# Handing the small products of a hybrid HGRN2 and retention layer to TensorE at other places in the program

## The chip, the cores and the metric

The kernel runs on one core of one Trainium2 chip. The core has TensorE (PE, matrix products), VectorE (DVE), ScalarE (ACT), GpSimd (POOL) and SyncE (SP, which here issues the DMAs). The time is device microseconds of the core for one execution of the whole program.

## The reference

One decoder layer over L = 2048 tokens of width D = 1024, in fp32. The hidden state is normalized and modulated by c, projected once into ten parts, and two recurrent mixers with 8 heads each work on them: HGRN2 (a linear recurrence with a decay f for each channel) and retention (a fixed decay for each head, with rotated q and k). Each output is normalized by head, gated, and the two are merged, projected back and added.

```python
mod = silu(c) @ w_ada + b_ada
shift, scale, gate = split(mod, 3)
h = rms_norm(x, norm_g) * (1 + scale) + shift
hq, hf, hi, hz, rq, rk, rv, rz, ga, gb = split(h @ w_in)
f = lb + (1 - lb) * sigmoid(hf);  k = 1 - f;  q = silu(hq)
oA: S_t = diag(f_t) S_(t-1) + k_t hi_t^T,   o_t = S_t^T q_t
oB: R_t = gamma R_(t-1) + rot(rk)_t rv_t^T, o_t = R_t^T rot(rq)_t
uA = head_rms_norm(oA) * silu(hz);  uB = head_rms_norm(oB) * silu(rz)
x = x + gate * ((sigmoid(ga) * uA + sigmoid(gb) * uB) @ w_out)
out = rms_norm(x, final_g)
```

## The kernel before

**Tiling.** The tokens are worked in NSB = 2 superblocks of 1024, each in two blocks of 512 or eight chunks of 128 (CH = 8). The heads go in NP = 4 pairs. For every superblock and pair PE runs dense projections in groups of 24 matmuls (8 steps along D, three matmuls of a split fp32 product each, `mm3`): `gf` and `gq` (weights a: f and q of HGRN2), `gr` (weights b: q and k of retention, for two pairs at once, so only in even pairs), `gv` (weights c: the values of both), `gg` (weights d: the gates). The first pair runs c, a, b, d; the others a, b (even pairs), c, d. At the end stands the output projection `ops`. Dense results go through three PSUM buffers (`gg0`, `gg1` ... name heads, the second number a chunk). Weights come by DMA (`wa` to `wd`, two raw tiles of 512 KB in flight); ACT copies the high part (`whd` ...), DVE subtracts the low part (`wld` ..., L464); `Ring` does both and keeps the last subtraction in `self.last`.

**Small products** are handed to PE between the dense ones. `Background` counts a tick at each step of three dense matmuls; after GAP = 9 ticks (27 dense matmuls) it makes a burst, in which each lane, a generator, may put its next piece: `tree` (L554) the seven levels `lv` 1, 2, 4 ... 64 of the products within a block of HGRN2, with the masked copies into `af`; `hgrn_out` (L683) the outputs and state updates `poh`; `retention` (L784) a chunk's scores `rt`, its output `por` and state. A lane that is not ready says so and the burst goes on without it. `bg.since` sets how far the count stands when a stage begins. `bg.post(w, fn)` calls fn w ticks later: it is used to issue DMAs when their operands should be there. `side` lanes (`block_r`, the row norms of a coming block) get a step every four ticks. PE keeps program order (`PE.on`); the other engines are ordered by the scheduler, unless `tc.issue_after(x)` puts instructions behind x on their engine.

**What the steps below touch.** After the last tree level, k times the decay is transposed on DVE (L645), stored to DRAM (`dk`, L657) and fetched back (`k<-dk`, eight DMAs, L650); `us` hands it to `hgrn_out` once `age[bb] + 6` ticks are past (L664). `rotate` (L742) turns q and k of a chunk: two multiplications that read the accumulator `gr` (L749), add and subtract (L757, L758), a transpose (L760), `kz` (L762), and `send`, which stores them 4 ticks later; it stands behind `ring.last`, the newest weight split. `retention` fetches them (`fetch`, L797, L798) up to one chunk ahead, again by a post of 4 ticks, into NQP = 3 buffers. `ada_row` (L176) makes a half of the output gate: eight multiply-adds on DVE (L189), then a matmul with ones, `gps`. `block_h` and `split_h` (L345) make the normalized h tiles of a block (high part L350 or L352, low part L353); those of block 2 are made while the last gates of superblock 0 run, in the `hook` (L1008) that is called behind each group. `gates` (L847) and `merge` (L857) are DVE's work behind each `gg` group.

## Time and profile before

| | |
|---|---|
| time, median of 3 runs | 2093.68 us (2092.19 to 2094.02) |
| the profiled execution's own time | 2095.28 us |
| span of its instructions | 2093.5 us |
| mean granted clock of PE | 0.992 |
| PE idle within the span | 2093.5 - 2039.0 = 54.5 us |
| DMA, mean over the span | 90 GB/s |

The busy time of an engine is what its records cover; a busy PE need not run at its full clock, so the clock granted to it is read beside it. In a list of waits, the engine named behind the arrow ended the wait. A row of the timeline gives the start, the length, the engine, the line, the operation, the result and operands, and in brackets the idle time of the engine before it with what ended it.

### The profile page before, as it was taken

Reading aid. Unit: us, or ns where it says so; the run is one execution under the profiler, and the core shown is the slowest. Engines: PE = TensorE matmul, PEld = TensorE weight load, DVE = VectorE, ACT = ScalarE, POOL = GpSimd, SP = SyncE. Lnnn points to the kernel's source line nnn. Section 1 sums busy time; section 2 is a strip of 40 time slices with the busy share of each in tenths; the row PEclk is TensorE's granted clock in tenths of the full one; section 3 lists DMA queues with packets and bytes.
Section 4 is the critical chain, followed back from the end, with each engine's and each line's share of the span. In section 5 each row is a group of like instructions: output and inputs, shape, how many; then the busy total and the mean of one; then the engine's idle time right before and its main releaser. Section 6 shows DMA issues by size and latency. Waiting matters only on the chain.

```text
span 2093.5 us, 38260 instructions
## 1 busy us (share of the span) xinstructions
PE 2039.0 (97%) x15448; PEld 1670.1 (80%) x15448; DVE 1086.0 (52%) x2435; ACT 572.5 (27%) x1389; POOL 145.9 (7%) x274
## 2 busy tenths in 40 slices
PE   6998999999999999999999999999999999999998
PEld 4786888788887887787888887888888887877886
DVE  7366544554365534556565544553464535465543
ACT  6312322322113221334213222322123222323221
POOL 1000100010000100121000100010000100110000
PEclk9999999999999999999999999999999999999999
DMA  8135221422244221435244221422344211447531
GB/s 314 41 75 124 63 72 46 93 57 56 60 118 96 68 54 47 103 93 154 56 102 97 67 55 46 97 56 53 73 99 94 72 47 53 100 113 203 176 131 60
DMA packets 312560, 187.66 MB, mean 90 GB/s; under 512 B 217664, under 2 KB 274496, under 8 KB 312384
## 3 DMA queue, kind: packets, MB, share of 16 engines
q1 hardware_dynamic: 312384, 185.22, 33.1%
q8 instruction: 121, 1.98, 0.4%
q14 instruction: 55, 0.45, 0.1%
HBM read 147.39 MB, written 37.75 MB: 88 GB/s over the span
## 4 chain that ended last, share of the span: by engine, by line
PE 52%; DMA 1%; DVE 1%; issue 1%; ACT 0%; POOL 0%; SPq 0%; DVEq 0%; POOLq 0%; ACTq 0%
PE gg L52 17%; PE gv L52 8%; PE ops L52 8%; PE gr L52 4%; PE gq L52 4%; PE gf L52 4%; PE poh L52 2%; PE lv L52 2%; PE por L52 1%; PE rt L52 1%; DMA wd<-in_w_d_dram 0%; DMA wc<-in_w_c_dram 0%; DMA mT_dram<-ga 0%; DMA wg<-in_w_gate_dram 0%; DMA wa<-in_w_a_dram 0%
## 5 line engine op out<-in xcount | busy, mean ns | idle before, releaser
L52 PE MATMUL gg<-whd,h 128*128 128x512 f32 x2048 | 658.6, 395 | 1.1 <-DVE tr L749 1.1
L52 PEld LDWEIGHTS gg<-whd,h 128*128 128x128 f32 x2048 | 386.6, 189 | 80.6 <-issue 1.9
L52 PE MATMUL gg<-wld,h 128*128 128x512 f32 x1024 | 400.3, 391 | 0.1
L52 PE MATMUL gv<-whc,h 128*128 128x512 f32 x1024 | 332.3, 397 | 3.5 <-ACT v L889 2.1
L52 PEld LDWEIGHTS gv<-whc,h 128*128 128x128 f32 x1024 | 192.5, 188 | 45.9 <-ACT v L889 3.3
L52 PEld LDWEIGHTS gg<-wld,h 128*128 128x128 f32 x1024 | 193.6, 189 | 38.8 <-DVE wld L464 0.5
L52 PE MATMUL gv<-wlc,h 128*128 128x512 f32 x512 | 199.0, 391 | 1.2 <-DVE wlc L464 1.1
L52 PE MATMUL gf<-h,wha 128*128 128x512 f32 x512 | 159.4, 392 | 2.4 <-DVE h L352 1.3
L52 PE MATMUL gr<-whb,h 128*128 128x512 f32 x512 | 160.3, 391 | 0.0
L52 PE MATMUL gq<-h,wha 128*128 128x512 f32 x512 | 158.6, 391 | 0.0
L52 PE MATMUL ops<-wo,mh 128*128 128x512 f32 x512 | 157.5, 389 | 0.0
L115 POOL TENSOR_TENSOR rrr<-ssr,mhalf 128x2 f32<-128x2 f32 x64 | 51.4, 803 | 1202.1 <-DVE ssr L114 1145.2
L850 ACT ACTIVATE sgg<-gg 128x512 f32<-128x512 f32 x128 | 74.8, 594 | 209.5 <-PE gg L52 206.9
L464 DVE TENSOR_TENSOR wld<-wd,whd 128x512 fp32r<-128x512 f32 x128 | 85.4, 683 | 69.4 <-ACT whd L463 69.3
L52 PEld LDWEIGHTS gf<-h,wha 128*128 128x128 f32 x512 | 96.4, 188 | 24.7 <-DVE h L353 2.5
L52 PEld LDWEIGHTS gv<-wlc,h 128*128 128x128 f32 x512 | 96.5, 189 | 20.8 <-DVE wlc L464 2.1
L52 PEld LDWEIGHTS gq<-h,wha 128*128 128x128 f32 x512 | 96.7, 189 | 20.1
L52 PEld LDWEIGHTS ops<-wo,mh 128*128 128x128 f32 x512 | 96.1, 188 | 20.0
L52 PEld LDWEIGHTS gr<-whb,h 128*128 128x128 f32 x512 | 96.1, 188 | 19.9
L675 ACT ACTIVATE jkh<-poh 128x128 f32<-128x128 f32 x128 | 35.4, 276 | 257.6 <-DVE st L725 212.6
L463 ACT ACTIVATE whd<-wd 128x512 fp32r<-128x512 f32 x128 | 79.3, 629 | 88.6 <-DMA wd<-in_w_d_dram 50.6
L853 DVE TENSOR_TENSOR ga<-gg,sgg 128x256 f32<-128x256 f32 x128 | 52.3, 414 | 93.1 <-ACT sgg L850 87.8
(160 smaller groups left out, 2799.9 us busy)
## 6 DMA issues: line engine op xcount, KB each, us to landing
wd<-in_w_d_dram SPq DMA_DIRECT2D x64, 512.0 KB, 3.8
wc<-in_w_c_dram SPq DMA_DIRECT2D x32, 512.0 KB, 3.8
wa<-in_w_a_dram SPq DMA_DIRECT2D x32, 512.0 KB, 3.8
wa<-in_w_ada_dram SPq DMA_DIRECT2D x16, 512.0 KB, 8.4
wb<-in_w_b_dram SPq DMA_DIRECT2D x32, 256.0 KB, 3.3
qkT<-tr SPq DMA_DIRECT2D x128, 64.0 KB, 2.0
rqk<-qkT SPq DMA_DIRECT2D x64, 128.0 KB, 2.3
dk<-f SPq DMA_DIRECT2D x16, 512.0 KB, 2.9
```

The lines of the kernel that those rows point to most:

```text
L52: made = nc.tensor.matmul(**kw)
L115: G.tensor_tensor(out=dst, in0=ss, in1=mhalf.broadcast_to([P, width]), op=ALU.pow)
L463: S.activation(out=hi, in_=w, func=AF.Copy)
L464: self.last = V.tensor_tensor(out=lo, in0=w, in1=hi, op=ALU.subtract).ins
L675: S.activation(out=junk, in_=pos[i], func=AF.Square, accum_out=ss[:, i : i + 1])
L850: S.activation(out=sg, in_=ps, func=AF.Sigmoid)
L853: V.tensor_tensor(out=ga, in0=ps[:, 0:256], in1=sg[:, 0:256], op=ALU.mult)
```

## The change

Seven edits, in the order of the diff. NQP grows to 4. `ada_row` gives up the turn three more times ahead of its matmul, with other numbers of steps in the hook. The high part of h is copied on ACT for blocks 2 and 3 too. `block_r` computes its row factor one step earlier and its matmul stands three steps behind and not two. `tree` hands its operands over 9 ticks after the fetch is issued (14 in the first pair of superblock 0). `rotate` is split: the multiplications stand behind the third newest weight split, the rest behind the newest, and for the last two chunks the rest follows after both multiplications. `retention` fetches up to two chunks ahead, at once, when the store was issued over 5 ticks ago. The first pair's retention may go only after `gr`, its first burst after it comes 12 ticks later than a full count, and odd pairs' first burst in `gv` 8 and not 5. `block_h(2)` starts behind chunk 3 with 3, 3 and 2 tiles.

```diff
@@ -29,7 +29,7 @@
 BLK = 512
 NBLK = SB // BLK
 CH = SB // P
-NQP = 3
+NQP = 4
 NV = 8
 NRAW = 2
 RING = 9
@@ -189,6 +189,8 @@
                     V.scalar_tensor_tensor(
                         out=acc, in0=w[:, i, :], scalar=sc[:, kt : kt + 1], in1=acc, op0=ALU.mult, op1=ALU.add
                     )
+            yield
+        for _ in range(3):
             yield
         ps = small_ps(f"gps{j}", "lv")
         PE.matmul(out=ps, lhsT=ones, rhs=acc, start=True, stop=True)
@@ -346,7 +348,7 @@
         hi, lo = pair_h(f"h{b}_{kt}", b % 2)
         h32 = upool.tile([P, 512], F32, name=f"h32_{b}_{kt}", tag="sg", bufs=3)
         S.activation(out=h32, in_=pre, func=AF.Identity, scale=amul[kt], bias=modp[kt])
-        if b == 0:
+        if b != 1:
             S.activation(out=hi, in_=h32, func=AF.Copy)
         else:
             V.tensor_copy(out=hi, in_=h32)
@@ -384,10 +386,10 @@
                 xt.append(upool.tile([P, 512], F32, name=f"xt{b}_{t}_{i}", tag="tr", bufs=3))
                 nc.sync.dma_start(out=xt[i], in_=a["x"][(4 * b + t) * P : (4 * b + t + 1) * P, i * 512 : (i + 1) * 512])
             yield
-            yield
             r = x_rstd(t, xt, f"b{b}_{t}")
             dg = upool.tile([P, P], F32, name=f"dgr{b}_{t}", tag="dgr", bufs=1)
             G.tensor_scalar(out=dg, in0=ident, scalar1=r, scalar2=None, op0=ALU.mult)
+            yield
             yield
             yield
             ps = small_ps(f"rb{b}_{t}", "lv")
@@ -438,6 +440,7 @@
             self.nsplit = 0
             self.nfree = 0
             self.ahead = NRAW
+            self.lasts = []
 
         def load(self, upto):
             while self.nraw < min(upto, len(self.pairs)):
@@ -461,7 +464,7 @@
                 hi = wpool.tile([P, 512], F32R, name=f"wh{key[0]}{i}", tag="whi", bufs=RING)
                 lo = wpool.tile([P, 512], F32R, name=f"wl{key[0]}{i}", tag="wlo", bufs=RING)
                 S.activation(out=hi, in_=w, func=AF.Copy)
-                self.last = V.tensor_tensor(out=lo, in0=w, in1=hi, op=ALU.subtract).ins
+                self.lasts.append(V.tensor_tensor(out=lo, in0=w, in1=hi, op=ALU.subtract).ins)
                 self.tiles[key, i % KT] = (hi, lo)
                 self.nsplit += 1
                 self.load(self.nsplit // 2 + self.ahead)
@@ -661,7 +664,7 @@
 
             bg.post(5.0 + 2.0 * bb, store)
         for bb in range(NBLK):
-            while bb not in age or bg.now < age[bb] + 6.0:
+            while bb not in age or bg.now < age[bb] + (9.0 if p or sb else 14.0):
                 yield True
             us[p, sb * NBLK + bb] = (q, kk, tl, f0)
             yield
@@ -737,10 +740,9 @@
 
 
 
-    turned_qk, rot = {}, {}
-
-    def rotate(p, gc, ps):
-
+    sent_qk, turned_qk, rot = {}, {}, {}
+
+    def rotate_products(p, gc, ps):
         nm = f"{p}_{gc}"
         qk = upool.tile([P, 512], F32, name=f"qk{nm}", tag="qk", bufs=2)
         tr = upool.tile([P, 512], F32, name=f"tr{nm}", tag="tr", bufs=3)
@@ -752,6 +754,11 @@
                 in1=tab[:, gc % CH * 32 : (gc % CH + 1) * 32].unsqueeze(1).broadcast_to([P, 16, 32]),
                 op=ALU.mult,
             )
+        return qk, tr
+
+    def rotate(p, gc, qk, tr):
+
+        nm = f"{p}_{gc}"
         qkv = qk.rearrange("p (g two d) -> p g two d", two=2, d=32)
         qsv = tr.rearrange("p (g two d) -> p g two d", two=2, d=32)
         V.tensor_tensor(out=qkv[:, :, 0, :], in0=qkv[:, :, 0, :], in1=qsv[:, :, 1, :], op=ALU.subtract)
@@ -777,7 +784,8 @@
                 )
             nc.sync.dma_start(out=dz, in_=kz)
             for w in range(2):
-                turned_qk[p + w, gc] = (dm[256 * w : 256 * w + 256], dz[:, P * w : P * w + P])
+                sent_qk[p + w, gc] = (dm[256 * w : 256 * w + 256], dz[:, P * w : P * w + P])
+                turned_qk[p + w, gc] = bg.now
 
         bg.post(4.0, send)
 
@@ -789,20 +797,18 @@
 
         def fetch(n):
             g = g0 + n
-            dm, dz = turned_qk[p, g]
+            dm, dz = sent_qk[p, g]
             qks[n] = upool.tile([P, 2, P], F32, name=f"rqk{p}_{g}", tag="rqk", bufs=NQP)
             kzs[n] = upool.tile([P, P], F32, name=f"rkz{p}_{g}", tag="rkz", bufs=NQP)
 
-            def load():
-                nc.sync.dma_start(out=qks[n], in_=dm.rearrange("(s p) t -> p s t", s=2))
-                nc.sync.dma_start(out=kzs[n], in_=dz)
-                age[n] = bg.now
-
-            bg.post(4.0, load)
+            nc.sync.dma_start(out=qks[n], in_=dm.rearrange("(s p) t -> p s t", s=2))
+            nc.sync.dma_start(out=kzs[n], in_=dz)
+            age[n] = bg.now
 
         n = nf = 0
         while n <= CH:
-            if nf < CH and nf <= n + 1 and (p, g0 + nf) in turned_qk:
+
+            while nf < CH and nf <= n + 2 and turned_qk.get((p, g0 + nf), bg.now) < bg.now - 5.0:
                 fetch(nf)
                 nf += 1
             if not go or n > len(vs) or (n < CH and (n not in age or bg.now < age[n] + 6.0)):
@@ -923,10 +929,16 @@
 
         def do_b(hook_last):
             if p % 2 == 0:
+                made = []
                 for c, ps in group_toks(sb, ("b", sb, p), f"gr{p}", 0, hook_last):
 
-                    with tc.issue_after(ring.last):
-                        rotate(p, sb * CH + c, ps)
+                    with tc.issue_after(ring.lasts[-3]):
+                        made.append((p, sb * CH + c, *rotate_products(p, sb * CH + c, ps)))
+                    if c != CH - 2:
+                        with tc.issue_after(ring.lasts[-1]):
+                            for m in made:
+                                rotate(*m)
+                        made = []
 
         def do_c():
             for c, ps in group_toks(sb, ("c", sb, p), f"gv{p}", len(vs)):
@@ -944,9 +956,10 @@
             do_c()
             bg.lanes.append(do_a())
             bg.since = GAP - 4.0
-            go.append(True)
             start_hgrn()
             do_b(start_ret)
+            go.append(True)
+            bg.since = GAP - 12.0
         else:
             made = do_a(start_ret if p % 2 else None)
             next(made)
@@ -954,7 +967,7 @@
             bg.lanes.append(made)
             start_hgrn()
             go.append(True)
-            bg.since = GAP - (5.0 if p % 2 else 12.0)
+            bg.since = GAP - (8.0 if p % 2 else 12.0)
             do_c()
         for j in range(2):
             h = h0 + j
@@ -1022,13 +1035,12 @@
                 pro["h"] = block_h(2 * sb + 2)
                 while 2 * sb + 2 not in rbs:
                     bg.force()
-            if c > 3:
-                steps(pro["h"], 2)
+            if c > 2:
+                steps(pro["h"], (3, 3, 2, 0, 0)[c - 3])
         if g == "g1" and p == NP - 1 and sb == NSB - 1:
             if c == 0:
                 pro["a"] = chain(ada_row(0), ada_row(1))
-            if c < 4:
-                steps(pro["a"], 2 if c else 4)
+            steps(pro["a"], (4, 2, 3, 3)[c] if c < 4 else 1)
             if c == 3:
                 pro["w"] = load_wo(0)
             if c > 3:
```

PE, superblock 0, pair 0, in the gates of head 0 (`gg0`): the first `poh` and the dense products ahead of it. Before:

```order
L52 MATMUL gg0_2_1973<-whd27_1711,h0_3_354 128x512
L52 MATMUL gg0_2_1973<-wld27_1712,h0_3_354 128x512
L52 MATMUL gg0_2_1973<-whd27_1711,h0_3_354 128x512
L52 MATMUL gg0_2_1973<-whd28_1723,h0_4_392 128x512
L52 MATMUL gg0_2_1973<-wld28_1724,h0_4_392 128x512
L52 MATMUL gg0_2_1973<-whd28_1723,h0_4_392 128x512
L52 MATMUL poh0_0_1991<-v0_0_627,k0_0_786 128x128
L52 MATMUL poh0_0_1991<-v0_0_627,af_109 128x128
L52 MATMUL poh0_0_1991<-v0_0_627,k0_0_786 128x128
L52 MATMUL poh0_0_1991<-v0_0_627,af_109 128x128
L52 MATMUL gg0_2_1973<-whd29_1733,h0_5_424 128x512
```

and with the change:

```order
L52 MATMUL gg0_4_2064<-whd30_1791,h1_6_599 128x512
L52 MATMUL gg0_4_2064<-wld30_1792,h1_6_599 128x512
L52 MATMUL gg0_4_2064<-whd30_1791,h1_6_599 128x512
L52 MATMUL rt0_3_2090<-rqk0_3_1964 128x128 x2
L52 MATMUL por0_2_0_2093<-rs0_121,rqk0_2_1613 128x128
L52 MATMUL por0_2_1_2094<-rs0_121,rqk0_2_1613 128x128
L52 MATMUL rt0_3_2090<-v0_2_631,rkz0_2_1614 64x128 x2
L52 MATMUL poh0_0_2102<-v0_0_627,k0_0_786 128x128
L52 MATMUL poh0_0_2102<-v0_0_627,af_109 128x128
L52 MATMUL poh0_0_2102<-v0_0_627,k0_0_786 128x128
L52 MATMUL poh0_0_2102<-v0_0_627,af_109 128x128
```

Before, `poh0_0` stood alone, 639 dense matmuls into the program, two bursts behind the last tree level `lv64` (585). Now it shares a burst with the fourth step of retention, at 693, and `lv64` stands at 612; the first `rt` of the pair moves from 585 to 612, the second, `rt0_1`, from 612 to 639.

DVE, in the same pair, where `gr` ends and `gg` begins; `wld` are weight splits, `qk0_6` and `tr0_6` the two multiplications of chunk 6. Before:

```order
L464 TENSOR_TENSOR wld30_1786<-wd3_3_1715,whd30_1785 128x512
L464 TENSOR_TENSOR wld31_1796<-wd3_3_1715,whd31_1795 128x512
L464 TENSOR_TENSOR wld32_1810<-wd4_0_1737,whd32_1809 128x512
L749 TENSOR_TENSOR qk0_6_1813<-gr0_6_1600,cos0_126 128x512
L749 TENSOR_TENSOR tr0_6_1814<-gr0_6_1600,sin0_128 128x512
L749 TENSOR_TENSOR qk0_7_1824<-gr0_7_1601,cos0_126 128x512
L757 TENSOR_TENSOR qk0_6_1813<-qk0_6_1813,tr0_6_1814 128x8x32
L758 TENSOR_TENSOR qk0_6_1813<-qk0_6_1813,tr0_6_1814 128x8x32
L749 TENSOR_TENSOR tr0_7_1825<-gr0_7_1601,sin0_128 128x512
L760 STREAM_TRANSPOSE tr0_6_1814<-qk0_6_1813 128x512
L762 TENSOR_TENSOR kz0_6_1820<-qk0_6_1813,zeta_107 128x256
```

and with the change:

```order
L467 TENSOR_TENSOR wld30_1792<-wd3_3_1723,whd30_1791 128x512
L467 TENSOR_TENSOR wld31_1802<-wd3_3_1723,whd31_1801 128x512
L751 TENSOR_TENSOR qk0_6_1817<-gr0_6_1600,cos0_126 128x512
L467 TENSOR_TENSOR wld32_1814<-wd4_0_1745,whd32_1813 128x512
L751 TENSOR_TENSOR tr0_6_1818<-gr0_6_1600,sin0_128 128x512
L751 TENSOR_TENSOR qk0_7_1821<-gr0_7_1601,cos0_126 128x512
L751 TENSOR_TENSOR tr0_7_1822<-gr0_7_1601,sin0_128 128x512
L764 TENSOR_TENSOR qk0_6_1817<-qk0_6_1817,tr0_6_1818 128x8x32
L765 TENSOR_TENSOR qk0_6_1817<-qk0_6_1817,tr0_6_1818 128x8x32
L764 TENSOR_TENSOR qk0_7_1821<-qk0_7_1821,tr0_7_1822 128x8x32
L767 STREAM_TRANSPOSE tr0_6_1818<-qk0_6_1817 128x512
```

The first multiplication of chunk 6 moved ahead of the split of weight 32, and both of chunk 7 ahead of the additions of chunk 6. In pair 2 the same happens with weight 96.

SP, superblock 0, pair 1, where k goes to DRAM and comes back (`dk1_0`, `k1_0`); `wd8` are gate weights, `rqk1` and `rkz1` retention's fetches. Before:

```order
L451 DMA wd8_0_3902<-in_w_d_dram 128x1024
L797 DMA rqk1_6_4010<-qkT0_6_1822 128x2x128
L798 DMA rkz1_6_4011<-kz0_6_1823 128x128
L657 DMA dk1_0_0_3944<-f1_0_2898 128x1024
L657 DMA dk1_0_1_3946<-f1_0_2898 128x1024
L451 DMA wd8_1_3975<-in_w_d_dram 128x1024
L650 DMA k1_0_2899<-dk1_0_0_3944 32x32x32 x4
L650 DMA k1_0_2899<-dk1_0_1_3946 32x32x32 x4
```

and with the change:

```order
L454 DMA wd8_0_3956<-in_w_d_dram 128x1024
L454 DMA wd8_1_3978<-in_w_d_dram 128x1024
L660 DMA dk1_0_0_4017<-f1_0_2898 128x1024
L660 DMA dk1_0_1_4019<-f1_0_2898 128x1024
L653 DMA k1_0_2899<-dk1_0_0_4017 32x32x32 x4
L653 DMA k1_0_2899<-dk1_0_1_4019 32x32x32 x4
```

The weight load `wd8_1` moved from between the store and the fetch to ahead of both, and retention's fetches are no longer among them: they were issued earlier.

In the other bursts the order changes thus: of the 56 bursts with a tree level 36 held a step of retention too, now 50; a program of 146 bursts has 149; 20 of them began with `lv` behind a dense matmul, now 6. In pairs 1 to 3 `lv64` and the first `poh` stay 54 dense matmuls apart. `gps0` moves from behind `gg7_9` to behind `gg7_10`, `gps1` from behind `gg7_11` to behind the last gate product, `gg7_15`.

## The prediction

> **What bounds the kernel now.** I read the busy times first, then what TensorE (PE) waited for, then the granted clock in short stretches, then the timeline around each wait. In the fences the busy line gives microseconds, share of the span and instruction count.
>
> ```profile
> PE 2039.0 (97%) x15448; PEld 1670.1 (80%) x15448; DVE 1086.0 (52%) x2435; ACT 572.5 (27%) x1389; POOL 145.9 (7%) x274
> ```
>
> PE is busy for 2039.0 of 2093.5 us, DVE for half of it. The change takes no matmul away, so what is to be had is the idle 54.5 us, the time in which PE ran at a lower clock, and small costs at switches. The waits of PE (what ran, what it waited for: us in all, times, longest):
>
> ```profile
> PE poh L52 <- DMA k<-dk: 9.9, 4, 5.5
> ...
> PE gps L52 <- DVE acc L189: 5.2, 2, 4.1
> PE lv L52 <- DVE qk L563: 4.1, 4, 1.1
> PE gv L52 <- ACT v L889: 2.1, 3, 0.7
> PE rt L52 <- DVE scm L829: 2.0, 1, 2.0
> ...
> PE gf L52 <- DVE h L352: 1.3, 1, 1.3
> PE gf L52 <- DVE h L353: 1.1, 3, 0.4
> PE gg L52 <- DVE tr L749: 1.1, 1, 1.1
> PE rb L52 <- POOL dgr L390: 0.8, 2, 0.5
> ```
>
> The rows left out belong to the start, which the change leaves alone, or are a few tenths. These nine rows sum to 27.6 us, and the change touches every one of them. The second loss is the clock: in these stretches PE was busy for nearly all the time that it had work, and the granted clock (the last number but two, 1.00 is full) was low.
>
> ```profile
> 200.00:206.00 6.00, 4.48 (x17) 4.00 (x18) 0.49 (x2) 0.74 (x4) 0.85 (x2) 0.72 0.82 101
> 410.00:416.00 6.00, 3.83 (x22) 3.05 (x21) 0.85 (x2) 0.03 (x1) 0.00 (x0) 1.00 1.12 126
> 416.00:420.00 4.00, 4.00 (x12) 3.15 (x12) 1.43 (x6) 1.14 (x5) 0.88 (x2) 0.57 0.22 35
> 977.00:990.00 13.00, 10.06 (x27) 5.98 (x26) 10.04 (x25) 7.18 (x14) 1.37 (x3) 0.74 0.68 209
> 1886.00:1891.00 5.00, 4.44 (x11) 3.19 (x12) 3.60 (x7) 1.67 (x3) 0.00 (x0) 0.66 0.42 120
> ```
>
> Each lies right behind one or more waits. Time lost is length times (1 - clock): 6 x 0.28 = 1.7, 4 x 0.43 = 1.7, 13 x 0.26 = 3.4, 5 x 0.34 = 1.7; 8.5 us together. What can go is therefore 27.6 + 8.5 = 36.1 us, and a little at switches. Next, wait by wait, whether it goes. A dense matmul starts every 0.227 us (648.23 to 648.45, below), so a burst distance of 27 is 6.1 us and a group of 24 is 5.45.
>
> **Pair 0: poh, rt, gg** (tree's later products, go after the rotations, rotation in two parts).
>
> ```profile
> 180.20 1.90 DVE L464 TENSOR_TENSOR wld<-wd,whd 128x512 fp32r<-128x512 f32 x3 [5.93 <-ACT whd L463]
> ...
> 188.40 0.49 PE L52 MATMUL rt<-rqk 64*128 64x128 f32 x4 [1.98 <-DVE scm L829]
> ...
> 195.53 6.05 SPq L650 DMA_DIRECT2D k<-dk x8
> ...
> 201.52 0.77 PE L52 MATMUL poh<-v,k 128*128 128x128 f32 x2 [5.46 <-DMA k<-dk]
> ```
>
> The first HGRN output (poh) waits for the fetch of k. Between the last tree products lv64 and poh stood two bursts (585 and 639 dense matmuls into the program), now there are three (612, 693): 6.1 us more than the wait's 5.46, and the row's 1.7 us of lost clock goes with it: **-7.2**. rt0_1 stood at 612, with its scm still behind the rotations on DVE; it moves to 639, 6.1 us for a wait of 1.98: **-2.0**. The gg wait of 1.1 comes from the rotation of chunk 6, queued behind three weight splits after an idle 5.93 us in which DVE waited for ACT. The new order puts one of its two multiplications ahead of the last split, and lv64's copies on ACT a burst later: I take **-0.8** (0 to 1.1).
>
> **poh in pairs 1, 2 and 3 of superblock 0.**
>
> ```profile
> 405.56 0.33 SPq L451 DMA_DIRECT2D wd<-in_w_d_dram  x1
> 406.54 8.48 SPq L650 DMA_DIRECT2D k<-dk x8
> ...
> 414.97 0.46 PE L52 MATMUL poh<-v,k 128*128 128x128 f32 x2 [2.17 <-DMA k<-dk]
> ...
> 667.06 6.61 SPq L650 DMA_DIRECT2D k<-dk x8
> ...
> 673.69 0.46 PE L52 MATMUL poh<-v,k 128*128 128x128 f32 x2 [0.81 <-DMA k<-dk]
> ...
> 871.13 7.68 SPq L650 DMA_DIRECT2D k<-dk x8
> ...
> 878.79 0.46 PE L52 MATMUL poh<-v,k 128*128 128x128 f32 x2 [1.43 <-DMA k<-dk]
> ...
> 665.31 0.39 PE L52 MATMUL por<-rs,rqk 64*128 64x128 f32 x4
> ...
> 666.00 0.71 PE L52 MATMUL por<-v,scm 128*128 128x128 f32 x4
> ```
>
> Here the later age (+9 ticks for +6) buys nothing: bursts come every 9 ticks, and lv64 to poh stays at 54 dense matmuls. Two other things help. In the same burst, ahead of poh, now stand the retention's last por and rt, which take 666.00 - 665.31 = 0.69 us. And in pairs 1 and 3 the store and the fetch of k had a 512 KB weight load between them in SP's queue (405.56); now that load goes ahead of both, so the fetch should take pair 2's 6.61 us instead of 8.48 and 7.68. What is left: 2.17 - 0.69 - 1.87 below zero; 0.81 - 0.69 = 0.12; 1.43 - 0.69 - 1.07 below zero. The margins are tenths. From the waits' 4.4 and the lost clock of 1.7 I take **-5.5**; bounds are 2.1 (only the 0.69 each) and 6.1.
>
> **First tree burst of odd pairs** (`since` GAP-8 for GAP-5).
>
> ```profile
> 346.39 0.27 PE L52 MATMUL lv<-qk,ones 128*32 128x32 f32 x8 [0.99 <-DVE qk L563]
> ```
>
> The first burst moves 9 dense matmuls (2.0 us) back, past the longest wait of 1.1; L563 itself does not move with it. All four go: **-4.1**.
>
> **gv in pair 2 and others** (rotations).
>
> ```profile
> 602.93 0.68 DVE L749 TENSOR_TENSOR tr<-gr,sin 128x512 f32<-128x512 f32 x1
> ...
> 603.44 0.50 PE L52 MATMUL gv<-whc,h 128*128 128x512 f32 x1 [0.69 <-ACT v L889]
> ```
>
> Before, gv's second accumulator was the one that ACT had just to empty. Now it is one that the rotation of chunk 6 frees with the multiplication at 602.93. The other multiplication moves ahead of a weight split, into DVE's wait for ACT, so this one runs about 0.6 us earlier: done near 603.0 where gv needs it at about 602.6. I take **-1.0** of the 2.1; the ends are 0 and 2.1.
>
> **Start of superblock 1** (block_h and block_r). Stretch 977 to 990 holds 13.00 - 10.06 = 2.9 us of waits for h and rb, and 3.4 of clock. The eight h tiles of block 2 are now made behind chunks 3 to 5 and not 4 to 7, two groups or 10.9 us earlier, against waits of at most 1.3. The cover is there:
>
> ```profile
> 955.00:966.00 11.00, 11.00 (x51) 9.11 (x50) 7.67 (x20) 4.38 (x8) 1.42 (x3) 1.00 0.55 156
> ```
>
> In the two groups before 966 DVE had 11.00 - 7.67 = 3.3 us free and ACT 6.6; the copies of hi that go to ACT add its time and take DVE's. **-6.0** of 6.3 (ends 2.9 and 6.3). If the cover fails, the weight splits on the same queues wait, and gg with them.
>
> **Gate row near the end** (ada_row).
>
> ```profile
> 1869.52 0.70 PE L52 MATMUL gps<-acc,ones 128*128 128x512 f32 x1 [1.14 <-DVE acc L189]
> ...
> 1886.56 0.70 PE L52 MATMUL gps<-acc,ones 128*128 128x512 f32 x1 [4.10 <-DVE acc L189]
> ...
> 1906.92 1.29 DVE L982 TENSOR_TENSOR wo<-wr,wo 128x512 fp32r<-128x512 f32 x2
> ...
> 1915.65 0.61 PE L52 MATMUL ops<-wo,mh 128*128 128x512 f32 x2
> ```
>
> gps0 moves one group back (5.45 against 1.14) and gps1 from behind group 11 to behind the last, while its operands move half a group: over 16 us against 4.10. Both waits and 1.7 of clock: **-6.9**. Row 1's work and so wo's may come a group later; wo's last pieces of the first half were ready at 1908.2 and first needed near 1915.7, which leaves 7.5 us for 5.45, so I add nothing.
>
> **Switches.**
>
> ```profile
> 648.23 0.39 PE L52 MATMUL gv<-wlc,h 128*128 128x512 f32 x1
> 648.45 0.39 PE L52 MATMUL gv<-whc,h 128*128 128x512 f32 x1
> 648.77 0.92 PE L52 MATMUL lv<-q,k 128*32 128x32 f32 x46
> ```
>
> A burst that begins with lv starts 0.32 us behind the last dense matmul, where 0.22 is the pace. 14 tree bursts get a retention product ahead of lv (20 begin with lv, then 6); three bursts are added. 14 x 0.09 = **-1.3**, ends 0 and -2.5. Retention's fetches are issued on SP without the 4 ticks' delay, the same count and bytes; a fourth buffer holds them; nothing waits for them now, so they are worth nothing either way, between -1 and +2 (a weight load behind them).
>
> **Sum**: 7.2 + 2.0 + 0.8 + 5.5 + 4.1 + 1.0 + 6.0 + 6.9 + 1.3 = 34.8 us. The profiled run took 2095.3 (span 2093.5 and 1.8 outside); it would take 2060.5. It lies 1.6 above the median of 2093.7, so against that median: 2058.9, said as **2059**, -1.7%.
>
> [...] At 414.97 PE had idled 2.17 us, and the clock of the next 4 us was 0.57: I book that loss to the wait. [...]
>
> **Rivals.**
>
> [...]
>
> *The waits only move*, so the change does not do what it says. poh in pairs 1 to 3 keeps its distance and its margins are tenths (5.5); gv now waits for the rotation (1.0); h's work earlier delays weight splits (3); the retention in each burst leaves por waiting for its scale by a few tenths in some of the 14 new places (3). Together +12.5: 2071. For it: bursts are 9 ticks apart whatever the age says. Against: most waits are cleared by whole microseconds.
>
> *Slower.* Retention steps now lie in 50 of 56 tree bursts, before in 36. If DVE cannot do a tree level and a retention step between two bursts, the next burst waits. To undo 34.8 us and add 0.2%, each of the 14 new ones must cost (34.8 + 4.2) / 14 = 2.8 us. It decides from the point at which DVE has more work for such a burst than the 6.1 us of dense matmuls behind it, and 2.8 us more work than that to bring the price.
>
> ```profile
> 636.00:644.00 8.00, 8.00 (x169) 6.48 (x168) 3.61 (x9) 4.69 (x10) 0.73 (x1) 1.00 0.10 29
> ```
>
> This stretch held a tree level with a retention step, and DVE was busy for 3.61 of 8; the fuller one above had 7.67 of 11. So the point is far. Passed by that much and a little, the time is 2100.
>
> *More than forecast*: everything goes, with the upper ends: 2053.
>
> **How the numbers follow.** Forecast 0.60 (2055 to 2063); clock stays 0.06; waits only move 0.18; slower 0.05; within 0.2% (which is about what a measurement of this kernel can tell from no change) 0.03, where both of the last happen in part; more than forecast 0.08. The range runs from 2052, below the upper ends, to 2076, which holds the moved waits with a third more; outside stay the slower cases and the worst of the moved ones. Faster 0.92, same 0.03, slower 0.05.
>
> **What would show it.** PE's list of waits without gps, lv for L563 and rt; poh's rows gone or below 0.3 us; stretches at full clock where 0.57 to 0.74 stood; gf at the start of superblock 1 without a wait; busy PE near 2030 of 2058. Wrong would be: poh's waits in pairs 1 to 3 still near 2 us, new waits of por or rt for DVE, gg or gv waiting for weight splits, ops for wo.

## The result, and the profile after

The changed kernel took 2056.12 us (median of 4 runs, 2055.40 to 2057.14), the kernel before beside it 2093.85 us (2092.19 to 2094.48). The ratio is 0.9821, 95% interval 0.9804 to 0.9838: faster by 37.7 us, or 1.8%. The forecast was 2059 in a range of 2052 to 2076. The profiled execution took 2056.69 us with a span of 2054.9, so 38.6 us less than the profiled one before.

The busy line of the page after, and PE's whole list of waits (what ran, what it waited for: us, times, longest):

```profile
PE 2026.3 (99%) x15448; PEld 1670.6 (81%) x15448; DVE 1080.5 (53%) x2419; ACT 579.8 (28%) x1405; POOL 147.8 (7%) x274
```

```profile
PE xps L56 <- ACT xt L362: 6.6, 4, 5.0
PE scp L52 <- DVE dgs L157: 5.9, 1, 5.9
PE gv L52 <- DVE tr L751: 2.1, 2, 1.0
PE xps L56 <- DVE xnf L364: 1.6, 2, 0.9
PE gv L52 <- ACT h L352: 1.4, 1, 1.4
PE gv L52 <- DVE wlc L467: 1.1, 1, 1.1
PE xps L56 <- ACT h L350: 0.9, 1, 0.9
PE por L52 <- issue: 0.3, 1, 0.3
PE ops L52 <- DVE wo L995: 0.2, 1, 0.2
```

The waits of poh for k, of gps, lv, rt, gf, gg and rb are gone from it. What is new is gv's wait for `tr`, the second multiplication of the rotation, 2.1 us where gv's wait for ACT had been 2.1. The rest is the start of the program, and a few tenths. The stretches of low clock are gone too; the same places, pair 1 and the long stretch from 975, with the granted clock as the last number but two:

```profile
190.00:206.00 16.00, 16.00 (x87) 12.58 (x86) 6.92 (x18) 2.67 (x10) 1.40 (x2) 1.00 0.72 157
955.00:968.00 13.00, 13.00 (x60) 10.77 (x59) 12.52 (x28) 8.76 (x15) 0.00 (x0) 1.00 0.45 134
1860.00:1870.00 10.00, 10.00 (x46) 8.29 (x45) 6.49 (x14) 4.99 (x9) 0.00 (x0) 1.00 0.79 224
...
395.00:420.00 25.00, 25.00 (x134) 20.42 (x133) 11.68 (x35) 4.91 (x20) 4.40 (x7) 1.00 0.47 99
975.00:2050.00 1075.00, 1069.15 (x7975) 883.68 (x7973) 555.77 (x1211) 277.12 (x680) 67.86 (x128) 1.00 0.33 90
```

PE busy is 2026.3, 12.7 us less than before for the same 15448 instructions. Lost clock hides in a busy time: in the stretch 416 to 420 of before, at a clock of 0.57, PE ran 12 matmuls in 4 us, where the pace of 0.227 us would give some 17. PE's idle time fell from 54.5 to 28.6 us.

Where the time went, from the start of the first `gf` of each superblock and pair in both timelines:

| stretch | change of its length, us | forecast for it |
|---|---|---|
| start, to the first `gf` | +1.0 | 0 |
| superblock 0, pair 0 | -10.9 | -10.0 |
| pair 1 | -5.5 | -4.9 |
| pair 2 | -2.4 | -1.1 |
| pair 3 | -4.1 | -2.4 |
| superblock 1, pair 0 | -7.6 | -6.3 |
| pair 1 | -1.5 | -1.0 |
| pair 2 | +0.7 | -0.3 |
| pair 3 | -9.5 | -7.9 |
| `ops` to the last of them | +1.6 | 0 |

(The forecast's single terms; its switches, -1.3, and its margin of 0.6 for poh lie over all pairs.) The eight pairs' stretches are 40.8 us shorter in all. PE's idle time in them fell by 25.9, and the four pieces of half clock (0.50), 17.1 us long in the trace of before, cost 8.5. Over 6 us are neither.

### The profile page after: what moved, and what is told of

Same layout as the page of the kernel before. It is cut to its first block, busy times and chain, and to the rows that moved or that the text cites. A ratio compares the mean times of both kernels' runs of the same rounds, so it can differ in the third digit from the quotient of the medians.

```text
span 2054.9 us, 38251 instructions
## 1 busy us (share of the span) xinstructions
PE 2026.3 (99%) x15448; PEld 1670.6 (81%) x15448; DVE 1080.5 (53%) x2419; ACT 579.8 (28%) x1405; POOL 147.8 (7%) x274
## 4 chain that ended last, share of the span: by engine, by line
PE 91%; DVE 3%; DMA 3%; issue 2%; SPq 1%; ACT 0%; POOL 0%; DVEq 0%; POOLq 0%; ACTq 0%
PE gg L52 31%; PE gv L52 16%; PE gq L52 8%; PE gf L52 8%; PE ops L52 8%; PE gr L52 7%; PE poh L52 4%; PE lv L52 3%; PE por L52 3%; PE rt L52 2%; DVE wa L169 1%; DMA wr<-in_w_o_dram 1%; DMA wc<-in_w_c_dram 1%; DVE wlc L467 0%; DMA wa<-in_w_ada_dram 0%
## 5 line engine op out<-in xcount | busy, mean ns | idle before, releaser
L115 POOL TENSOR_TENSOR rrr<-ssr,mhalf 128x2 f32<-128x2 f32 x64 | 54.5, 852 | 1216.0 <-DVE ssr L114 1104.5
L52 PE MATMUL gr<-wlb,h 128*128 128x512 f32 x256 | 99.9, 390 | 0.0
```

The lines of the kernel that those rows point to most:

```text
L52: made = nc.tensor.matmul(**kw)
L115: G.tensor_tensor(out=dst, in0=ss, in1=mhalf.broadcast_to([P, width]), op=ALU.pow)
```

## The experiments

Each kernel was run in turns with the kernel before, which had medians of 2095.7 to 2096.7 beside them; beside the first run of the changed kernel it had 2093.85. The 2 us that the next text puts down to the chip are this difference; no run shows that the chip makes it.

**The changed kernel again.**

> The changed kernel itself once more, beside the kernels of this call, since chips differ by some 2 us for the same kernel: 2055 to 2059. Its trace shows whether gv's waits for the rotation in even pairs, 1.0 and 1.0 us in its first profile, stay of that size.

2055.69 us (2055.42 to 2056.94), ratio 0.9806 (0.9791 to 0.9821), here 41.0 us less than the kernel before. gv's waits for the rotation were 1.5 us in all and ops waited 1.1 us for wo. The experiments below that undo one part are held against 2056.

**Retention's early fetches undone.**

```diff
-NQP = 4
+NQP = 3
-            while nf < CH and nf <= n + 2 and turned_qk.get((p, g0 + nf), bg.now) < bg.now - 5.0:
+            if nf < CH and nf <= n + 1 and (p, g0 + nf) in turned_qk:
...
+            bg.post(4.0, load)
```

> The changed kernel with retention's fetches as before (three buffers, one chunk ahead, issued by a post of 4 ticks); all else as changed. Theory: poh in pairs 1 to 3 of superblock 0 no longer waits because retention's last products stand ahead of it (0.69 us) and because the weight load went ahead of the store of k, and both come from the earlier fetches. Then the waits of poh for k come back in pairs 1 to 3, near 2.2, 0.8 and 1.4 us, with some 1.7 us of half clock behind the longest, and 1.3 to 3 us of switches: 2056 + 8 = 2064, 2062 to 2066. poh of pair 0 stays without a wait. Rival: the age of 9 ticks is what clears them: no wait comes back, only switches do, 2057 to 2059.

2066.82 us (2062.57 to 2069.90), some 11 us more. The timeline's rows of PE at the first poh of pairs 1 to 3, at two row norms of the next block, and at one tree level of pair 1 in superblock 1:

```profile
404.03 0.46 PE L52 MATMUL poh<-v,k 128*128 128x128 f32 x2 [1.41 <-DMA k<-dk]
...
658.88 0.46 PE L52 MATMUL poh<-v,k 128*128 128x128 f32 x2 [0.92 <-DMA k<-dk]
...
864.51 0.46 PE L52 MATMUL poh<-v,k 128*128 128x128 f32 x2 [1.38 <-DMA k<-dk]
...
877.69 0.46 PE L52 MATMUL rb<-dgr,ones 128*128 128x128 f32 x2 [0.84 <-DVE v L681]
...
897.14 0.46 PE L52 MATMUL rb<-dgr,ones 128*128 128x128 f32 x2 [2.22 <-DVE v L681]
...
1266.64 0.31 PE L52 MATMUL lv<-q,k 128*32 128x16 f32 x14 [2.30 <-issue]
```

poh's waits are back, 3.7 us, so the age is not what clears them. The program itself says so too: built with 6 in place of 9 outside the first pair it is the same, instruction for instruction, so that edit does nothing (the 14 of the first pair was not taken apart). But the theory was half wrong. SP's rows have the weight load ahead of the store of k here as well, and the fetch took 7.0 us; that half is not the fetches' doing. And rb waits 3.1 us, with 1.7 us of half clock behind the second, which neither theory had; the experiment after the next shows where that comes from. A last part of the 11 us, 2.3 of wait and 1.7 of half clock, is the `lv` shown, which waited for nothing that the profile shows. It isn't shown that the fetches have a part in it, so what they are worth is less sure than the median says.

**Odd pairs' first burst after 5 ticks.**

```diff
-            bg.since = GAP - (8.0 if p % 2 else 12.0)
+            bg.since = GAP - (5.0 if p % 2 else 12.0)
```

> The changed kernel with the first burst of odd pairs after 5 ticks and not 8. Theory: the four waits of lv for qk, about 1.0 us each, come back: +3.5 to +4.5. Rival: the wait came from the weight splits ahead of qk on VectorE, which run earlier now, so that it comes back by half or less: +0 to +2.

2063.88 us (2063.23 to 2065.50), some 8 us more, twice the theory. lv's waits came back with 4.7 us, and poh's with them. The timeline of SP and PE in pair 1, of this kernel first:

```profile
397.13 1.45 SPq L660 DMA_DIRECT2D dk<-f  x2
398.83 0.33 SPq L454 DMA_DIRECT2D wd<-in_w_d_dram  x1
399.87 8.13 SPq L653 DMA_DIRECT2D k<-dk  x8
...
407.95 0.46 PE L52 MATMUL poh<-v,k 128*128 128x128 f32 x2 [1.08 <-DMA k<-dk]
```

and of the changed kernel:

```profile
397.74 1.45 SPq L660 DMA_DIRECT2D dk<-f  x2
400.45 6.90 SPq L653 DMA_DIRECT2D k<-dk  x8
...
407.12 0.44 PE L52 MATMUL rt<-v,rkz 128*64 128x128 f32 x4
407.49 0.49 PE L52 MATMUL poh<-v,k 128*128 128x128 f32 x2
```

The three ticks decide whether the weight load falls between the store and the fetch of k: with it the fetch took 8.13 us, without it 6.90, and poh's 1.08 of wait is about that difference (in pair 3 it took 8.18 for 6.65, and poh waits 1.05). Together with the kernel above this takes apart the two halves that the forecast named for poh: the retention products ahead of it come from the early fetches, the shorter fetch from the three ticks, each worth 1.0 to 1.4 us of poh's wait in pairs 1 and 3.

**The three ticks alone, in the kernel before.**

> The kernel before with one part of the change alone: the first burst of odd pairs after 8 ticks and not 5. Theory: these three ticks do two things, they take away the four waits of lv for qk (4.1 us), and they put a weight load ahead of the store of k in SP's queue in pairs 1 and 3, so that the fetch of k takes some 6.9 us and not 8.5 and 7.7 and poh waits there 0.5 to 1.3 us and not 2.2 and 1.4; the half clock behind the longest wait goes with it: -6 to -8 us against the kernel before. Rival: lv's waits alone go, poh's stay as they were: -3.5 to -4.5.

2097.87 us (11 runs) against 2096.43, ratio 1.0009 (1.0000 to 1.0018): nothing gained, and both theories fell. Its waits, with the two groups of interest, and the stretch behind the second rb:

```profile
PE poh L52 <- DMA k<-dk: 9.5, 4, 5.9
...
PE rb L52 <- DVE ssr L114: 3.1, 2, 2.2
```

```profile
891.51 0.46 PE L52 MATMUL rb<-dgr,ones 128*128 128x128 f32 x2 [0.86 <-DVE ssr L114]
...
910.98 0.46 PE L52 MATMUL rb<-dgr,ones 128*128 128x128 f32 x2 [2.25 <-DVE ssr L114]
```

```profile
911.00:915.00 4.00, 4.00 (x12) 3.19 (x13) 1.35 (x5) 0.28 (x1) 0.78 (x1) 0.57 0.16 40
```

lv's waits for qk are gone, and the fetches of k took 6.9 and 7.0 us, as the theory has it; poh's waits in pairs 1 to 3 fell from 4.4 to 3.6 us. But the row norms `rb` of the next block keep their place while the bursts move by 9 dense matmuls, and the first rb now stands 9 of them behind `poh3_1`, where it had stood 18. It takes over the accumulator of that poh, and so waits until DVE has read it: 3.1 us and 4 x 0.43 = 1.7 of clock. In the program of the changed kernel the same rb waits for POOL alone, since retention is done by then and the poh ahead of it takes an accumulator of another pool. Two things more went against the gain in this profile, neither explained: an `lv` of superblock 1 waited 1.5 us for nothing that the profile shows, and the half clock at the start of superblock 1 lasted 10.2 us for 6.8 before.

**The three ticks and the early fetches, in the kernel before.**

> The kernel before with two parts of the change: the first burst of odd pairs after 8 ticks, and retention's earlier fetches (four buffers, two chunks ahead, without the post). Theory: the three ticks alone gain nothing since rb of pair 3 then comes 9 dense matmuls behind a poh whose accumulator it takes, and waits 1.0 and 2.4 us with half clock behind; with retention done earlier rb takes another accumulator, and these waits are gone. Then lv's waits (4.1 us) and poh's in pairs 1 to 3 (4.4 and 1.7 of clock) are gained whole, and some switches: -11 to -13, near 2084.5 where the kernel before has 2096.4; the first pair loses as much as before, some 10 us, in other waits. Rival: rb's waits stay, or the first pair gets worse: -5 to -8.

2084.55 us (2083.47 to 2090.21), ratio 0.9944 (0.9930 to 0.9959). That is the 11 us of the theory. The profiled execution, the slowest of the five with 2090.21, shows the waits: rb only 1.0 us for POOL, poh 1.2, lv 0.5. So the three ticks gain their waits only with the early fetches. The fetches alone were not tried in the kernel before.

**The first pair as before.**

```diff
-            start_hgrn()
-            do_b(start_ret)
-            go.append(True)
-            bg.since = GAP - 12.0
+            go.append(True)
+            start_hgrn()
+            do_b(start_ret)
...
-            while bb not in age or bg.now < age[bb] + (9.0 if p or sb else 14.0):
+            while bb not in age or bg.now < age[bb] + 9.0:
```

> The changed kernel with the first pair's bursts as before (retention may go before the rotations are done, no 12 ticks of delay, operands handed over at an age of 9). The last tree level and the first poh stand at 585 and 639 dense matmuls, as before. Theory: the wait of that poh for k comes back, 3 to 5 us, with 1.7 us of half clock, and so do the waits for the rotations by 1 to 3 us: +5 to +9 against the changed kernel, 2061 to 2065. Rival: with two retention steps ahead of it and fewer transfers in SP's queue the fetch is done in time: +0 to +2.

2067.93 us (2067.25 to 2068.59), 12 us more, over both ranges, and by another mechanism. In the profile 10.8 of it are in the first pair. PE's timeline in that pair, and DVE's around it:

```profile
190.27 0.80 PE L52 MATMUL rt<-rqk 64*128 64x128 f32 x4 [2.21 <-issue]
193.84 1.13 PE L52 MATMUL por<-rs,rqk 64*128 64x128 f32 x4 [2.77 <-DVE v L681]
...
205.53 0.49 PE L52 MATMUL poh<-v,k 128*128 128x128 f32 x2
```

```profile
189.56 0.41 DVE L835 TENSOR_TENSOR scm<-rt,dT 128x256 f32<-128x256 f32 x1
189.89 0.28 DVE L838 COPY rs<-rt 128x128 f32<-128x128 f32 x1
190.09 1.21 DVE L609 TENSOR_TENSOR q<-q,f 128x1024 f32<-128x1024 f32 x1
191.22 1.22 DVE L610 TENSOR_TENSOR k<-k,f 128x1024 f32<-128x1024 f32 x1
...
193.44 0.35 DVE L681 SCALAR_TENSOR_TENSOR v<-por,rrr,gr 128x128 f32<-128x128 f32 x1 [0.51 <-POOL rrr L115]
```

This poh does not wait at all (one of pair 2 waits 1.2 us). Retention's steps, early through the new fetches, run into the rotations. The rt shown needs its accumulator back from DVE's scm and rs, which stand behind the rotations and end at 190.17; the profile names no releaser, but the program has it wait for rs. por needs an accumulator that DVE's L681 has to read, and this stands behind the last tree level's two products (L609, L610). Half clock follows from 190.04 to 200.28, which is 5.1 us lost. So the delay of the first pair is what keeps the early fetches from harm there. This is the mechanism of the forecast's slower rival, a tree level and a retention step that DVE cannot do between two bursts; in the changed kernel it shows nowhere.

**The gate row as before.**

```diff
-        for _ in range(3):
-            yield
...
-            steps(pro["a"], (4, 2, 3, 3)[c] if c < 4 else 1)
+            if c < 4:
+                steps(pro["a"], 2 if c else 4)
```

> The changed kernel with the gate row's matmuls where they stood before (no extra turns, old steps). Theory: the two waits of gps for acc come back at about 1.1 and 4.1 us, and a stretch of half clock behind the second: +7 to +8, 2063 to 2064; ops at the end does not wait for wo any more (0.2 to 1.5 us less). Rival: with the other parts changed DVE is ahead of where it was, so that the waits are under half of those: 2058 to 2060.

2064.34 us (2062.06 to 2065.92), 8 us more. The timeline's two rows of gps:

```profile
1841.40 1.10 PE L52 MATMUL gps<-acc,ones 128*128 128x512 f32 x2 [2.29 <-DVE acc L189]
1857.27 1.41 PE L52 MATMUL gps<-acc,ones 128*128 128x512 f32 x2 [2.95 <-DVE acc L189]
```

Divided otherwise than before (1.14 and 4.10), the same 5.2 us; 3.41 us of half clock follow the second. The mechanism of the theory holds, and ops' waits went, as expected. Its size does not follow from the 8 us: in this profile gv waits 2.1 us for the rotation at the start of superblock 1, with half clock behind it, and that pair, which the edit does not touch, is 3.0 us longer than in the changed kernel. The gate row's own pair is 8.2 us longer and ops' stretch 1.6 shorter, 6.5 together.

**h of block 2 as before** (and the row norms' steps).

```diff
-            if c > 2:
-                steps(pro["h"], (3, 3, 2, 0, 0)[c - 3])
+            if c > 3:
+                steps(pro["h"], 2)
...
-        if b != 1:
+        if b == 0:
```

> The changed kernel with h of block 2 made behind chunks 4 to 7 and its high part copied as before, and the row norms' steps as before. Theory: the waits of gf and rb at the start of superblock 1 come back, 2.5 to 3 us, with 3 us of half clock: +5 to +6.5 against the changed kernel. Rival: the earlier retention has freed VectorE and ScalarE there, so that h is ready anyway: +0 to +1.5.

2065.47 us (2061.79 to 2066.68). The stretch 955 to 968 again, in this kernel:

```profile
955.00:968.00 13.00, 10.54 (x27) 6.20 (x26) 9.98 (x25) 7.11 (x13) 1.37 (x3) 0.66 0.68 208
```

2.5 us of waits and a clock of 0.66 are back, as the theory has it, but the 9.5 us are more than its 6.5. In the profile the first pair of superblock 1 is 7.9 us longer than in the changed kernel's first one, half clock from 959.11 to 969.35 among it, and pair 2 is 2.1 us shorter, where gv waits less. This profiled execution was the fastest of the four; where the other three lost some 4 us more can't be seen in it and stays open.

**The rotation in one part**, behind the newest weight split.

> The changed kernel with the rotation in one part, behind the newest weight split, as before. PE's program is the same. Theory: the first multiplication no longer fills DVE's wait for ACT, so gv's second accumulator in even pairs comes 0.6 us later where DVE waits there, and the first gate of pair 0 waits for its rotation by up to 1 us: +1 to +2.5, 2057 to 2058.6. Rival: the split decides nothing, 2056 within 0.5.

2058.53 us (2056.93 to 2064.36): at the upper end of the theory's range and with a wide spread. Its profile is of the slowest of the four: gv's waits for the rotation are 3.9 us for 2.1, one of 1.9 has half clock behind it, and `gg`'s in pair 0 is back with 0.6 us. I read it as 1 to 2.5 us, not as settled.

**The rotation further ahead**, and **with wo's loads earlier.**

```diff
-                    with tc.issue_after(ring.lasts[-3]):
+                    with tc.issue_after(ring.lasts[-4]):
...
-            steps(pro["w"], 2)
+            steps(pro["w"], 1 if t else 3)
```

> The changed kernel with the rotation's two multiplications one weight split further ahead on VectorE (behind the fourth newest split and not the third newest). Theory: gv's second accumulator waits for the second multiplication because that stands behind a split that waits for a weight; ahead of that split it runs in VectorE's idle time, and gv's waits for the rotation go to zero without a new one: 2 to 3.5 us less than the changed kernel on the same chip, 2053 to 2055. Rival: the splits behind it come late instead, gv waits for wlc by as much, and the time is the changed kernel's within 0.7.

> The changed kernel with the rotation's multiplications behind the fourth newest weight split, and three of the four loads of the second half of the output weights issued behind the first output group (two before). Theory: gv's waits for the rotation (1.5 to 2.1 us) and ops' waits for wo (about 1.1 us) go: 2053 to 2054, some 2.5 us under the changed kernel. Rival: the loads of x behind that weight load in SP's queue come late and VectorE holds up the outputs, or contention eats it: 2055 to 2057.

2055.23 us (2053.85 to 2056.31) with the first edit alone and 2054.77 us (2053.78 to 2056.01) with both, where the changed kernel had 2055.69. The ratios to the kernel before are 0.9802 (0.9788 to 0.9817) and 0.9802 (0.9788 to 0.9815), the changed kernel's 0.9806. The traces show the waits for the rotation gone and spans of 2053.2 and 2053.0 for 2055.2, but by the times neither is told apart from the changed kernel. Of the theory's 2 to 3.5 us the median shows 0.5.

**Twelve pauses.** In the second head's gates of pairs 0 to 2 a small matmul was made to wait for a chain of n + 1 copies on ACT, n = 1 to 23:

```python
PE.matmul(out=ps[:, 0:8], lhsT=ones, rhs=pt, start=True, stop=True)
S.activation(out=pt, in_=ps[:, 0:8], func=AF.Copy, scale=0.5)
for _ in range(n):
    S.activation(out=pt, in_=pt, func=AF.Copy, scale=0.5)
...
PE.matmul(out=ps[:, 0:8], lhsT=ones, rhs=pt, start=True, stop=True)
```

> The changed kernel with twelve pauses of PE added among the gates of the second head in pairs 0 to 2, each a small matmul that waits for a chain of 2 to 24 small copies on ScalarE; the result of the layer is not touched. It measures how long a wait must be to cost clock. Theory from the profile of before: behind waits from about 2 us on the granted clock falls to about half for some 4 us (1.7 us lost each), behind those up to 1.5 us it does not. [...] Waits should run from about 0.8 to 6 us in steps of 0.4; the time is 2056 + 40 of waits + 8 to 14 of clock.

2123.54 us, one run. Two of the pauses in the timeline:

```profile
473.33 0.39 PE L52 MATMUL pb<-pt,ones 128*128 128x8 f32 x2 [2.28 <-ACT pt L1030]
...
734.48 0.39 PE L52 MATMUL pb<-pt,ones 128*128 128x8 f32 x2 [2.79 <-ACT pt L1030]
```

The shorter one cost clock and the longer one did not. The trace's record of the clock tells them apart. In it half clock (0.50) begins at 276.12, 474.09, 494.57, 757.40 and so on, whole multiples of 3.413 us apart: 474.09 to 494.57 is 6 times that, 494.57 to 757.40 is 77 times. Behind a pause it lasts 3.41 or 6.83 us. In the trace of before it begins at 201.37, 416.41, 983.02 and 1887.56, which are 63, 166 and 265 times 3.413 us apart, and lasts 3.41, 3.41, 6.83 and 3.41 us. I call a stretch of 3.413 us between two such times a slot. The time around the two pauses, slot by slot:

```profile
470.68:474.09 3.41, 1.13 (x8) 0.95 (x7) 1.80 (x6) 2.18 (x11) 0.92 (x2) 1.00 0.10 14
474.09:477.50 3.41, 3.41 (x9) 2.67 (x8) 1.35 (x6) 0.00 (x0) 0.00 (x0) 0.50 0.22 53
477.50:481.00 3.50, 3.50 (x17) 2.85 (x16) 0.00 (x0) 0.07 (x1) 0.00 (x0) 1.00 0.16 23
...
730.09:733.50 3.41, 1.60 (x9) 1.27 (x7) 2.32 (x8) 1.71 (x8) 0.83 (x2) 1.00 0.07 10
733.50:736.91 3.41, 2.43 (x12) 2.05 (x13) 0.99 (x3) 0.83 (x4) 0.00 (x0) 1.00 0.25 38
736.91:740.32 3.41, 3.41 (x23) 3.05 (x22) 0.61 (x2) 0.74 (x4) 0.25 (x2) 1.00 0.02 2
```

The first number is the slot's length, the second PE's busy time. The pause of 2.28 us lies in one slot, 3.41 - 1.13 = 2.28 idle, and the next slot is at 0.50. The pause of 2.79 us falls into two, 1.81 and 0.98 idle, and the clock stays at 1.00. All twelve:

| PE idle, us | 0.81 | 1.35 | 2.28 | 2.76 | 2.79 | 3.28 | 3.76 | 4.23 | 4.71 | 5.19 | 5.67 | 6.15 |
|---|---|---|---|---|---|---|---|---|---|---|---|---|
| most of it in one slot, us | 0.81 | 1.35 | 2.28 | 2.59 | 1.81 | 2.15 | 2.44 | 2.25 | 2.68 | 3.37 | 3.41 | 3.41 |
| half clock behind it, us | 0 | 0 | 3.41 | 3.41 | 0 | 3.41 | 6.83 | 6.83 | 6.83 | 3.41 | 6.83 | 6.83 |

In the traces of before and after, from 100 us on to 15 us before the end, three slots at full clock held 1.97 us of idle time or more (1.97, 2.41 and 3.41), and half clock began behind each. Behind the 1135 with 1.5 us or less it never began. Of three between, it began behind the one of 1.63 and not behind those of 1.69 and 1.90. Counted over all fourteen traces of this case, those of the experiments among them, there are 23 slots with 1.97 us or more and half clock behind each, none behind the thousands with 1.5 us or less, and twelve between, 1.55 to 1.90 us, with half clock behind five. Short waits in one slot added up: the slot ahead of the half clock at 983.02 in the kernel before, 979.61 to 983.02, has 1.63 us of idle time, from waits of at most 1.3.

So the theory is not right as it stood. In these traces the idle time in a slot, not the length of a wait, tells whether half clock follows: 2.28 us in one slot had it behind them, 2.79 us over two slots (1.81 and 0.98) had not.

## Why the prediction was right, point by point

- **Only waits and clock can be had: right.** PE's instructions are as many, idle fell by 25.9 us and busy time by 12.7, of which half clock in the pairs explains some 8.
- **Pair 0, 10.0 us: right**, 10.9 measured. All three waits went. What the undone part showed is that it holds only as a whole: with the early fetches and without the delay the pair loses as much as before, in the waits of rt and por for DVE and the half clock behind them.
- **poh in pairs 1 to 3, 5.5: right**, and in its two halves (retention products ahead, weight load ahead): waits 4.4 and clock 1.7 went to nothing. That the age does nothing there was right too.
- **lv in odd pairs, 4.1: right.** In pair 1 of superblock 1, which had no other wait, the stretch is 1.5 us shorter.
- **gv, 1.0: wrong.** The step that failed is that the first multiplication "moves ahead of a weight split, into DVE's wait for ACT", so that the second runs 0.6 us earlier. It does so in superblock 0, where the wait is gone. In superblock 1 DVE's rows leave no such wait to fill, and gv waits for the same multiplication:

```profile
1503.26 0.69 DVE L751 TENSOR_TENSOR qk<-gr,cos 128x512 f32<-128x512 f32 x1
1503.86 0.68 DVE L467 TENSOR_TENSOR wld<-wd,whd 128x512 fp32r<-128x512 f32 x1
1504.46 0.69 DVE L751 TENSOR_TENSOR tr<-gr,sin 128x512 f32<-128x512 f32 x1
```

```profile
1505.29 0.47 PE L52 MATMUL gv<-whc,h 128*128 128x512 f32 x1 [1.02 <-DVE tr L751]
```

- **Start of superblock 1, 6.0: right**, 7.6 with a gv wait that only changed its cause; the undone part gave 7.9 in this stretch of its profile.
- **Gate row, 6.9: right within its pair, but a cost was put at nothing.** gps' 5.2 us of waits and the 1.7 of half clock, which lay from 1887.56 to 1890.97, are gone, and so are lv's 1.1. The pair is 9.5 us shorter; 1.3 of that are neither idle time nor clock. Against it stands wo, for which nothing was added: ops' stretch is 1.6 us longer, though not at its first half but 20 us later. Little of this shows as PE's waits, 0.3 us; its weight loads for ops wait 1.5 us for wo, where no such wait was before. The undone part gave 6.5 for both together.
- **Switches, 1.3: too low for what it has to cover.** Over 6 us in the eight pairs are neither idle time nor half clock. A part may come with each wait that went: in the timeline a dense matmul lasts 0.39 us and one starts every 0.227, so by my estimate a wait hides some 0.16 us more in the busy time, 3 us for some 20 waits fewer. No run took this apart, so what the switches gave stays open.
- **The rivals.** That the waits only move was true of gv alone. The clock, to whose staying low the forecast gave 0.06, came back with the waits: from 57 to 2049 us the profile after has no half clock. The losses of 1.7 us at 416 and 3.4 us from 983 fit what the pauses showed, with 1.97 us idle in the slot ahead of the one and 1.63 in the slot ahead of the other. Slower did not happen, but its mechanism exists, one part away.

The forecast's 34.8 us against 37.7 (38.6 in the two profiles) is thus good in its waits and clock, 33.5 forecast and 34.4 measured. The rest is two misses that partly cancel, and that is luck: over 6 us neither wait nor clock, where 1.3 were forecast for switches, and 2.6 us lost at the start and in ops, where nothing was (the 1.0 of the start is not in the changed kernel's second profile).

## What to carry to other kernels

Where products are handed over on a fixed raster, a part that moves the raster need not be worth the waits that it removes: it also decides which load falls between a store and its fetch, and which accumulator the next user finds. Undo parts one at a time from the whole and try them alone: here one part was worth 8 us in the whole and nothing by itself. And read the clock behind the waits, since nearly half of a loss may stand in the busy time: here 2.17 us of wait cost 1.7 us of clock.

## What the runs showed of the hardware

In the traces of the kernel before and of the pauses the granted clock of PE fell to 0.50 for 3.41 or 6.83 us behind slots with idle time, at times that lie multiples of 3.413 us apart within each trace. In the kernel before, 1.97 us of idle time from 413.00 to 416.41 were followed by 3.41 us at 0.50; 1.90 us from 194.55 to 197.96 were not. Among the twelve pauses, 2.28 us of waiting within one slot cost clock, and 2.79 us over two slots did not. With a load of 512 KB issued on SP between the store of k and the eight DMAs of its fetch, these took 8.13 us in pair 1 (odd pairs' first burst after 5 ticks); in the changed kernel, with that load ahead of the store, 6.90.
